# A decoder layer's down projection for two of three token groups, done as seven block products

## The chip, the cores and the metric

One core of one Trainium2 chip. The metric is the device time of one execution in microseconds (us), as the median of several runs. A profile of one execution stands beside it; its "span" runs from the first to the last instruction of the program.

## What is computed

One decoder layer over 1056 tokens (1024 of a prompt, 32 of eight decoded sequences), width 1024, in float32. In short, from the reference:

```python
h = _rms(x, n_mix_pre); z = h @ w_in                     # q, k, v, pooling input
mix = concat([attention(q, k, v), pooling(u)]) @ w_out
x = x + _rms(mix, n_mix_post)
f = _rms(x, n_ffn_pre)
f = (silu(f @ w_gate) * (f @ w_up)) @ w_down             # 1024 -> 2816 -> 1024
x = x + _rms(f, n_ffn_post)
x = x + sigmoid(x @ w_ple_gate) * (p @ w_ple)            # "PLE", p has 256 columns
```

The change concerns `@ w_down`: 2816 hidden columns, which are 22 chunks of 128, times a 2816 x 1024 matrix.

## The kernel before

**Layout.** Activations lie transposed: 128 partitions are 128 columns of the model, and the free dimension holds tokens. The tokens are three groups (0, 1, 2) of 352. A tile of half a group's state is 128 x 4 x 352 = 128 x 1408 elements. All such tiles come from one pool of 27 slots (`act_tile`, `half`, `A_SLOTS`).

**Precision.** Each operand X is split into hi (a rounded copy, made by ScalarE, line 171) and lo (X - hi, made by VectorE, line 172); a product takes three matmuls, hi·hi + hi·lo + lo·hi (`gemm`). One matmul is 128 x 128 weights against 128 x 352 tokens.

**Weights.** `w_load` brings raw weights (512 KB, 128 x 1024) on SP's DMA queue into one of three raw tiles (`wr`, `W_RAW`). Splits go into eight tiles (`wp`). The list ITEMS holds all weights of the feed-forward part in the order of use; `need(k)` makes item k and those up to four ahead (`LOOK`). An item is "direct" (split all of it: `wh`, `wl`), "half" (split its second half: `w`), "small" (for the PLE embedding) or "sums" (below).

**Groups 0 and 1 together ("the pair").** Their gate, up and PLE gate products are already done in a seven-product form of a 2 x 2 block matrix product (Winograd's variant of Strassen's). The weights are four blocks of 4 x 128 rows; the tokens four blocks (two halves of the rows by two groups). `w_sums` (line 1025) makes the weight blocks' four sums on POOL, in place in the raw tiles; then ScalarE and VectorE split them (`sh`, `sl`). `f7` holds seven token operands B11, B21, B22 and T1 to T4, each as hi and lo (14 tiles). `seven` runs the products one after another, 12 matmuls into one PSUM bank each, and VectorE adds the banks up into the four results C11, C12, C21, C22. With eight PSUM banks, TensorE stops when VectorE is too late. For a chunk, seven products make gate and up for both groups: 84 matmuls where the plain way takes 96.

**Group 2** goes the plain way (`direct`: 24 matmuls into one bank).

**Order.** TensorE's instructions stay in the order of the program from line 988 on; a scheduler orders the other engines' instructions when the program is built, and each engine then takes its own in that order. WALK is the list of (slab, groups), a slab being two chunks: six slabs of group 2, eleven slabs of the pair, the other five of group 2. For each slab gate and up of its chunks are made; the hidden values are split into `hid` (`hid_put`); and inside the next slab's first chunk `downs` runs the slab's down products: for each group and each of eight output blocks m, six matmuls (two chunks, three each) into a bank, which VectorE adds to the output tile `os_` (line 1130, the first time ScalarE copies). That is 22 x 8 x 3 = 528 matmuls for a group.

**Chains.** The work between the big products (norms, residual sums, the making of `f7`, of `fs[2]` for group 2, of `x27` and `x2s` for PLE) is written as generators (`ffn_steps`, `pair_steps`, `one_steps`), which `turn` advances between products by estimated costs, so that it lies beside the products. `t_sum` (line 984) makes T1 to T4 from the state on POOL, `sum_halves` (line 357 to 360) and `squares_into` (line 816) the sums of squares, for groups 0 and 1 on POOL. `finish` runs what is left of a chain.

**The PLE stage** has four steps of seven products for the pair (`ple_pair`), the last down products of group 2 after the first of them, and then eight plain steps for group 2 (`ple_one`).

Of the kernel before, what the change touches and what calls it, by code (L numbers as in the profile page):

```python
# [10 lines left out]
F32 = mybir.dt.float32  # L11
# [5 lines left out]
P = 128  # L17
# [19 lines left out]
SLAB = 2  # L37
NSLAB = FFC // SLAB

AHEAD = 6  # L40
# [17 lines left out]
A_SLOTS = 27  # L58
# [3 lines left out]
def trunk_kernel(  # L62
# [9 lines left out]
    w_dn,  # L72
    w_pg,
# [145 lines left out]

    WALK = [(s, (2,)) for s in range(AHEAD)]  # L220
    WALK += [(s, (0, 1)) for s in range(NSLAB)]
    WALK += [(s, (2,)) for s in range(AHEAD, NSLAB)]
    LAST = {g: max(n for n, (_, gs) in enumerate(WALK) if g in gs) for g in range(G)}
# [6 lines left out]
    def direct_item(src, shape):  # L230
        return item("direct", add_plan(src, shape))
# [4 lines left out]
    def half_item(src):  # L236
        return item("half", add_plan(src, [P, KC, P]))

    def dn_items(n):
        return [direct_item(w_dn[WALK[n][0], j], [P, SLAB, 512]) for j in range(2)]  # L240

    WGU, WD = [], []
    for s, gs in WALK:
        pairs_of = []
        for i in range(SLAB):
            c = SLAB * s + i
            jg = direct_item(w_gu[c, 0], [P, KC, P])
            if 0 not in gs:
                ju = direct_item(w_gu[c, 1], [P, KC, P])
            if i == 0 and WD:  # L250
                WD[-1] = dn_items(len(WD) - 1)
            if 0 in gs:
                ju = half_item(w_gu[c, 1])
            js = item("sums", jg, ju) if 0 in gs else None
            pairs_of.append((jg, ju, js))
        WGU.append(pairs_of)
        WD.append(None)


    WP2, WPE = [], [None] * KC  # L260
    for i in range(KC // 2):
        jg = direct_item(w_pg[2 * i], [P, KC, P])
        ju = half_item(w_pg[2 * i + 1])
        js = item("sums", jg, ju)
        WP2.append((small_item(w_ple[i]), jg, ju, js))
        if i == 0:
            WD[-1] = dn_items(len(WALK) - 1)
    wp = WP2[-1][0]
    LATE = (6, 7, *range(6))
    for m in LATE:  # L270
        if m < 6 and m % 2 == 0:
            wp = small_item(w_ple[m // 2])
        WPE[m] = wp, direct_item(w_pg[m], [P, KC, P])
# [47 lines left out]
    def rstd_steps(acc):  # L321

        n = acc.shape[1]
        sm = bank()
        for i in range(TB):
            at = min(i * P, n - P)
            mm(sm[:, i : i + 1], acc[:, at : at + P], ones[:, 0:1], start=True, stop=True)
        sd = spool.tile([P, TB], F32, tag="sd", name=nm("sd"))  # L330
        fix(se.activation(sd, sm[:, :TB], AF.Sqrt, bias=epst, scale=1.0 / D))
        fix(ve.reciprocal(sd, sd))
        hl = spool.tile([P, 2, TB], F32R, tag="hl", name=nm("hl"))
        fix(ve.tensor_copy(hl[:, 0], sd))
        fix(ve.tensor_tensor(hl[:, 1], sd, hl[:, 0].bitcast(F32), op=ALU.subtract))
        dgs = []
        for h in range(2):
            dg = spool.tile([P, TB, P], F32R, tag="dg", bufs=4, name=nm("dg"))
# [12 lines left out]
    def acc_tile(g):  # L351
        return spool.tile([P, NS[g]], F32, tag=f"acc{g}", bufs=1, name=nm("acc"))

    def sum_halves(sqs, g, eng=ve):

        a, b = sqs
        fix(eng.tensor_tensor(a, a, b, op=ALU.add))
        fix(eng.tensor_tensor(a[:, 0:2, :], a[:, 0:2, :], a[:, 2:4, :], op=ALU.add))
        acc = acc_tile(g)
        fix(eng.tensor_tensor(acc, a[:, 0, :], a[:, 1, :], op=ALU.add))  # L360
        return acc
# [23 lines left out]
    xs, acc1, r1 = [[None] * 2 for _ in range(G)], [None] * G, [None] * G  # L385
# [18 lines left out]
    def x_sums(g):  # L404
        acc1[g] = sum_halves([xr[g, h] for h in range(2)], g)
# [402 lines left out]
    acc = [acc_tile(g) for g in range(G)]  # L808
# [119 lines left out]
    def ffn_steps(g):  # L928
# [8 lines left out]
        acc2 = sum_halves(ys[g], g, ve if g == 2 else ge)  # L937
        yield (20, 6) if g == 2 else (0, 45)
        r = yield from rstd_steps(acc2)
        for h in range(2):  # L940
# [32 lines left out]
    f7 = {}  # L973

    def t_sum(name, b7, c0, c1, to):
# [8 lines left out]
        ge.tensor_tensor(out, a, b, op=ALU.subtract)  # L984
# [22 lines left out]

    hid = [None] * G

    new_hid = [None] * G  # L1010

    def hid_put(g, slot, ht):
        split(new_hid[g][:, slot, :], new_hid[g][:, SLAB + slot, :], ht)

# [41 lines left out]
    def seven(items, x7, done):  # L1056

        ig, iu, is_ = items
# [21 lines left out]
    def gate_up_pair(items, slot, pending):  # L1080
# [3 lines left out]
        def done(which, c):  # L1084
# [3 lines left out]
            if which == "C11":  # L1088
                if pending:
                    pending()  # L1090
                for g in (0, 1):
                    if slot == 0:
                        new_hid[g] = half(g, F32R, "hid")
            for g, a, b in ((0, "C21", "C11"), (1, "C22", "C12")):
                if which == ("C21", "C12")[g]:
                    ve.tensor_tensor(t[a], t[a], t[b], op=ALU.mult)
                    hid_put(g, slot, t[a])

        seven(items, f7, done)

    def gate_up_one(items, slot, pending):
        ig, iu, _ = items
        wg = need(ig)
        sl = tmp(N, "sl")
        se.activation(sl, direct(wg, fs[2]), AF.Silu)
        wu = need(iu)
        ve.tensor_tensor(sl, sl, direct(wu, fs[2]), op=ALU.mult)
        if slot == 0:
            new_hid[2] = half(2, F32R, "hid")
        hid_put(2, slot, sl)  # L1110
        if pending:
            pending()

    os_ = [None] * G

    def down(n, m, g):
        wh, wl = need(WD[n][m // 4], 0 if n == len(WALK) - 1 else LOOK)
        cols = slice((m % 4) * P, (m % 4 + 1) * P)
        ps = bank()
        v = ps[:, : NS[g]]  # L1120
        gemm(v, [(wh[:, k, cols], wl[:, k, cols], hid[g][:, k, :], hid[g][:, SLAB + k, :]) for k in range(SLAB)])
        turn(6)
# [3 lines left out]
        if (g, m) not in begun:  # L1126
            begun.add((g, m))
            se.copy(o, v)
        else:
            ve.tensor_tensor(o, o, v, op=ALU.add)  # L1130

    begun = set()
    x2 = [[None] * 2 for _ in range(G)]
# [3 lines left out]
    acc3 = [None] * G  # L1137
    x2d = [[dpool.tile([P, 4, NS[g]], F32, name=nm("x2d")) for _ in range(2)] for g in range(2)]

    def last_down(n, m, g):  # L1140
        down(n, m, g)
        if m == 0:
            acc3[g] = acc_tile(g)
        squares_into(acc3[g], os_[g][m // 4][:, m % 4, :], m == 0, ve if g == 2 else ge)
# [47 lines left out]
    def downs(n):  # L1192
        gs = WALK[n][1]
        hid[:] = old_hid
        for half_m in (range(4), range(4, KC)):
            for g in gs:
                for m in half_m:
                    (last_down if n == LAST[g] else down)(n, m, g)
        if n == LAST[0]:
            share[0] = 0.5  # L1200
            chain(pair_steps(), 19)
        if n == LAST[2]:
            chain(one_steps(), 40)

    for n, (s, gs) in enumerate(WALK):
        if n == AHEAD:
            finish(list(chains))
        old_hid = list(new_hid)
        for i in range(SLAB):
            pending = (lambda: downs(n - 1)) if i == 0 and n else None  # L1210
            (gate_up_pair if 0 in gs else gate_up_one)(WGU[n][i], i, pending)
    finish(list(chains))
    share[0] = 0.5


# [15 lines left out]
    def ple_pair(i):  # L1231

        wp, *items = WP2[i]
# [5 lines left out]
        def done(which, c):  # L1239
# [3 lines left out]
            embed(wp, xm[g][:, m % 4, :], m, g, c)  # L1243
# [3 lines left out]
    def ple_one(m):  # L1247
        wp, w = WPE[m]
# [4 lines left out]
    old_hid = list(new_hid)  # L1253
    for i in range(KC // 2):
        ple_pair(i)
        if i == 0:
            downs(len(WALK) - 1)
    finish(list(chains))
    for m in LATE:
        ple_one(m)  # L1260
# [14 lines left out]
def _layout(i):  # L1275
# [28 lines left out]
        "w_dn": wd.reshape(NSLAB, SLAB, P, 2, 512).transpose(0, 3, 2, 1, 4),  # L1304
# [43 lines left out]
```

## Time and profile before

| | |
|---|---|
| median of 3 runs | 1118.83 us (1117.93 to 1118.85) |
| the profiled execution | 1120.06 us |
| its span | 1117.9 us |
| TensorE's granted clock, mean | 0.997 |
| matmuls | 7099 |
| POOL's sums of weights (line 1025) | 104 of 1.30 to 1.36 us |
| loads of weights for w_gate, w_up, w_down | 132 of 512 KB, 3.3 us each |

How to read the profile: PE is TensorE's matmuls, PEld its weight loads, DVE is VectorE, ACT ScalarE, POOL GpSimd, SP the queue that issues most DMAs. A row of a group gives line, engine, operation, output tile <- input tiles, shapes, count, then busy us, mean ns of one, and the idle time just before them with what ended it. A row of a wait gives who waited for what: us in total, times, longest. A row of the timeline gives start, length, engine, line, operation and, in brackets, the idle time before it. Matmuls overlap in the profile, so that the time of one says less than their number in a stretch.

### The profile page before, as it was taken

The page shows a single profiled execution, that of the slowest core. Times are in us where ns is not written, and L with a number is a line of the kernel's source. Part 1 is how long each engine was busy: PE and PEld are TensorE (multiplying, and loading weights), DVE is VectorE, ACT ScalarE, POOL GpSimd, SP SyncE. Part 2 cuts the span into 40 slices and gives each one's busy share as a digit, 9 for nine tenths or more (in the row PEclk, how much of TensorE's full clock was granted, in tenths as well). Part 3 has the DMA queues.
Part 4 walks back from the last instruction along what each step waited for, and adds up shares of the span by engine and source line. Part 5 has one row for each costly group of instructions (what it writes and reads, how often), then busy time and mean ns, then how long its engine had stood idle before and what let it go on. Part 6 is the DMA issues. An engine that isn't in the chain of part 4 may idle for free.

```text
span 1117.9 us, 18031 instructions
## 1 busy us (share of the span) xinstructions
PE 1102.0 (99%) x7099; PEld 1084.3 (97%) x7099; DVE 818.8 (73%) x1298; ACT 476.6 (43%) x834; POOL 259.7 (23%) x200
## 2 busy tenths in 40 slices
PE   9999999999999999999999999999999999998998
PEld 8999988899999999999999999999999999998998
DVE  6766478877989957477677677677677788867973
ACT  7322377665555433533233233233233644443441
POOL 0054132100223212212212212212211503113200
PEclk9999999999999999999999999999999999999999
DMA  8121311542543333222122222122123555472261
GB/s 288 57 70 57 108 57 32 202 146 93 183 168 132 116 101 105 68 85 76 66 86 77 66 86 76 65 87 76 63 90 100 185 191 210 133 254 75 94 206 64
DMA packets 42421, 125.53 MB, mean 112 GB/s; under 512 B 4932, under 2 KB 15460, under 8 KB 42336
## 3 DMA queue, kind: packets, MB, share of 16 engines
q1 hardware_dynamic: 41008, 122.61, 32.4%
q10 hardware_dynamic: 1328, 1.77, 0.5%
q8 instruction: 56, 0.92, 0.3%
q14 instruction: 29, 0.24, 0.1%
HBM read 111.37 MB, written 12.99 MB: 111 GB/s over the span
## 4 chain that ended last, share of the span: by engine, by line
PE 93%; DVE 4%; DMA 2%; POOL 1%; issue 1%; ACT 0%; SPq 0%; DVEq 0%; POOLq 0%; ACTq 0%
PE b L126 92%; DVE wl L172 1%; PE b L120 1%; DMA a<-in_dmask_dram 1%; POOL wr L1025 0%; DVE fl L172 0%; DVE hid L172 0%; DMA xr<-in_x_dram 0%; DMA wr<-in_w_gu_dram 0%; DVE dg L340 0%; DVE acc L816 0%; DVE mx L659 0%; DVE a L767 0%; DVE o L1130 0%; DVE y L944 0%
## 5 line engine op out<-in xcount | busy, mean ns | idle before, releaser
L126 PE MATMUL b<-hid,wh 128*128 128x352 f32 x1056 | 252.6, 322 | 1.6 <-DVE hid L172 1.2
L172 DVE TENSOR_TENSOR wl<-wr,wh 128x1024 fp32r<-128x1024 f32 (+1 forms) x148 | 195.7, 1323 | 43.5 <-ACT wh L171 33.6
L171 ACT CAST wh<-wr 128x1024 fp32r<-128x1024 f32 (+1 forms) x148 | 152.4, 1031 | 159.0 <-PE b L126 108.7
L126 PE MATMUL b<-fh,wh 128*128 128x352 f32 x624 | 202.7, 325 | 2.5 <-DVE o L1130 2.5
L126 PE MATMUL b<-fh,wl 128*128 128x352 f32 x624 | 201.2, 322 | 0.0
L126 PE MATMUL b<-fl,wh 128*128 128x352 f32 x624 | 201.0, 322 | 0.0
L126 PEld LDWEIGHTS b<-hid,wh 128*128 128x128 f32 x1056 | 182.7, 188 | 2.3 <-DVE hid L172 1.5
L126 PE MATMUL b<-hid,wl 128*128 128x352 f32 x528 | 169.3, 321 | 0.0
L1025 POOL TENSOR_TENSOR wr<-wr 128x512 f32<-128x512 f32 x52 | 67.8, 1303 | 431.2 <-DVE w L172 373.7
L126 PE MATMUL b<-fh,sh 128*128 128x352 f32 x416 | 134.3, 323 | 0.0
L126 PE MATMUL b<-fl,sh 128*128 128x352 f32 x416 | 133.4, 321 | 0.0
L126 PE MATMUL b<-fh,sl 128*128 128x352 f32 x416 | 133.4, 321 | 0.0
L1130 DVE TENSOR_TENSOR o<-o,b 128x352 f32<-128x352 f32 x240 | 112.7, 517 | 14.6 <-PE b L126 14.4
L126 PEld LDWEIGHTS b<-fh,wh 128*128 128x128 f32 x624 | 117.7, 189 | 3.1 <-DVE o L1130 3.1
L126 PEld LDWEIGHTS b<-fl,wh 128*128 128x128 f32 x624 | 118.1, 189 | 0.0
L126 PEld LDWEIGHTS b<-fh,wl 128*128 128x128 f32 x624 | 117.8, 189 | 0.0
L171 ACT CAST sh<-wr 128x1024 fp32r<-128x1024 f32 x52 | 54.2, 1045 | 131.3 <-POOL wr L1025 129.9
L126 PE MATMUL b<-h,wh 128*128 128x352 f32 x480 | 104.9, 324 | 1.0 <-ACT h L392 0.8
L172 DVE TENSOR_TENSOR sl<-wr,sh 128x1024 fp32r<-128x1024 f32 x52 | 63.6, 1223 | 56.0 <-ACT sh L171 54.5
L126 PEld LDWEIGHTS b<-hid,wl 128*128 128x128 f32 x528 | 99.1, 188 | 0.0
L126 PEld LDWEIGHTS b<-h,wh 128*128 128x128 f32 x480 | 81.5, 188 | 2.2 <-ACT h L392 1.1
L126 PEld LDWEIGHTS b<-fl,sh 128*128 128x128 f32 x416 | 78.2, 188 | 0.0
(173 smaller groups left out, 1890.1 us busy)
## 6 DMA issues: line engine op xcount, KB each, us to landing
wr<-in_w_gu_dram SPq DMA_DIRECT2D x88, 512.0 KB, 3.3
wr<-in_w_dn_dram SPq DMA_DIRECT2D x44, 512.0 KB, 3.3
wr<-in_w_pg_dram SPq DMA_DIRECT2D x16, 512.0 KB, 3.6
x<-in_x_dram SPq DMA_DIRECT2D x6, 704.0 KB, 7.6
x1d<-x SPq DMA_DIRECT2D x6, 704.0 KB, 3.4
x<-x1d SPq DMA_DIRECT2D x6, 704.0 KB, 6.5
out_y_dram<-yo SPq DMA_DIRECT2D x24, 176.0 KB, 1.9
wr<-in_w_out_b_dram SPq DMA_DIRECT2D x8, 512.0 KB, 3.3
```

The lines of the kernel that those rows point to most:

```text
L120: ins = te.transpose(out, src, ident)
L126: ins = te.matmul(*args, **kw)
L171: fix(se.copy(hi, src))
L172: fix(ve.tensor_tensor(lo, src, hi.bitcast(F32), op=ALU.subtract))
L1025: ge.tensor_tensor(out, a, b, op=op)
L1130: ve.tensor_tensor(o, o, v, op=ALU.add)
```

## The change

A slab is now four chunks, five slabs and a rest of two chunks (`REST`). The order is written out as a list STEPS of small steps.

- **Pair's down products.** For the pair a slab's hidden values are kept in float32 (`hidf`); when the slab's four chunks are there, `h_operands` makes seven operands `h7` from them (128 x 2 x 352 each; four sums and seven splits). The slab's down weights are, for each half j of the outputs, two raw tiles of 512 KB in the block order that `seven_items` takes: one direct, one half, one sums. `do_dn_pair` runs seven products for each j, each as two groups of 6 matmuls, and adds each into one of seven accumulators of its own (`accp`), in which all five slabs are summed up; so the combination of the seven into the four results is made once, at the end, by seven additions of 128 x 1408 on VectorE (`do_combine`). `do_dn_pair` of a slab stands after the second and third chunk of the next slab. The rest of two chunks goes the plain way (`do_dn_rest`).
- **Group 2's down products** take four chunks into a bank (12 matmuls), so that there is one addition to `os_` where there were two.
- **Group 2's state away.** Its normed state is stored to DRAM (`fsd`) when it is made, its partial output (`osd`) after its third slab; both are loaded again behind the pair's chunks, and the state split anew (`do_reload`, `do_reload_sums`). The pool of tiles has 30 slots; the tiles for sums of squares (`acc_rows`) and for the norm's diagonal (`dg2`) come from it.
- **Sums on VectorE.** `t_sum`, `sum_halves` and `squares_into` of groups 0 and 1 run on VectorE in place of POOL.

Group 2 has twelve chunks before the pair and ten behind it, as it had.

```diff
-SLAB = 2
+SLAB = 4
 NSLAB = FFC // SLAB
-AHEAD = 6
+REST = FFC - SLAB * NSLAB
+AHEAD = 3
-A_SLOTS = 27
+A_SLOTS = 30
...
+    for s in range(AHEAD):
+        for i in range(SLAB):
+            s_one(s, i)
+            if s:
+                s_dn_one(s - 1, i)
+    step("spill")
+    for s in range(NSLAB):
+        for i in range(SLAB):
+            s_pair(s, i)
+            if s == 0 and i < 2:
+                s_dn_one(AHEAD - 1, 2 * i, 2 * i + 1)
+                if i == 1:
+                    step("spill_sums")
+            if s and i in (1, 2):
+                s_dn_pair(s - 1, i - 1)
+    s_pair(NSLAB, 0)
+    s_pair(NSLAB, 1)
+    step("reload")
+    for j in range(2):
+        s_dn_pair(NSLAB - 1, j)
+    step("combine")
+    for s in range(AHEAD, NSLAB):
+        for i in range(SLAB):
+            s_one(s, i)
+            if s > AHEAD:
+                s_dn_one(s - 1, i)
+            if (s, i) == (AHEAD, 1):
+                s_dn_rest(0, 1)
...
-        acc2 = sum_halves(ys[g], g, ve if g == 2 else ge)
+        sum_halves(ys[g], acc[g])
...
+                    nc.sync.dma_start(fsd[h], ys[g][h])
...
-        ge.tensor_tensor(out, a, b, op=ALU.subtract)
+        ve.tensor_tensor(out, a, b, op=ALU.subtract)
...
+    def h_operand(name, src):
+        t = act_tile([P, 2, 2, N], F32R, "hp")
+        split(t[:, 0], t[:, 1], src)
+        h7[name] = t[:, 0], t[:, 1]
+
+    def h_sum(name, out, a, b):
+        ve.tensor_tensor(out, a, b, op=ALU.subtract)
+        h_operand(name, out)
+
+    def h_operands():
+        b11, b21, b12, b22 = (hidf[g][:, 2 * k : 2 * k + 2, :] for g in (0, 1) for k in range(2))
+        h_operand("B11", b11)
+        h_operand("B21", b21)
+        h_operand("B22", b22)
+        h_sum("T1", b11, b12, b11)
...
+    def do_dn_pair(s, j, items):
+        ia, ib, is_ = items
+        for at, which, h, x in (
+            (1, ia, 0, "B11"),
+            (2, ia, 1, "B21"),
+            (4, ib, None, "T4"),
+            (6, is_, "S2", "T2"),
+            (7, is_, "S3", "T3"),
+            (5, is_, "S1", "T1"),
+            (3, is_, "S4", "B22"),
+        ):
...
+            for r in range(2):
+                ps = bank()
+                gemm(ps[:, :N], [(w[0][:, 2 * c + r, :], w[1][:, 2 * c + r, :], xh[:, c, :], xl[:, c, :]) for c in range(2)])
+                turn(6)
+                o = accp[at][:, 2 * j + r, :]
+                if s:
+                    ve.tensor_tensor(o, o, ps[:, :N], op=ALU.add)
+                else:
+                    se.copy(o, ps[:, :N])
+
+    def do_combine():
+        for a, b in ((2, 1), (1, 6), (7, 1), (1, 5), (1, 3), (4, 7), (7, 5)):
+            ve.tensor_tensor(accp[a], accp[a], accp[b], op=ALU.add)
+        os_[0] = [accp[2], accp[4]]
+        os_[1] = [accp[1], accp[7]]
...
+    def do_reload():
+        for h in range(2):
+            t = half(2, s="fr")
+            nc.sync.dma_start(t, fsd[h])
+            fs[2][h] = f_operand(t, 2)
```

More of the change, by code (lines that the diff above doesn't have):

```diff
@@ L260, in trunk_kernel, with seven_items, step, s_one @@
-    WP2, WPE = [], [None] * KC
+    def seven_items(a1, a2, small=None):
+        jg = direct_item(a1)
+        more = () if small is None else (small_item(small),)
+        ju = half_item(a2)
+        return (jg, ju, item("sums", jg, ju), *more)
+    STEPS = []
+    def step(kind, *args):
+        STEPS.append((kind, args))
+    def s_one(s, i):
+        c = SLAB * s + i
+        step("one", s, i, (direct_item(w_gu[c, 0]), direct_item(w_gu[c, 1])))
+    def s_pair(s, i):
+        c = SLAB * s + i
+        step("pair", s, i, seven_items(w_gu[c, 0], w_gu[c, 1]))
@@ L404, in x_sums @@
     def x_sums(g):
[L405 removed]
+        sum_halves([xr[g, h] for h in range(2)], acc1[g])
     def u_load(c, h):
@@ L806, in out_pool @@
         se.copy(ys[g][0][:, m, :], ps[:, : NS[g]])
-    acc = [acc_tile(g) for g in range(G)]
+    acc = acc_rows()
     def squares_into(acc_g, src, first, eng=ve):
@@ L973, in trunk_kernel @@
     f7 = {}
+    fsd = [dpool.tile([P, 4, N], F32, name=nm("fsd")) for _ in range(2)]
     def t_sum(name, b7, c0, c1, to):
@@ L1136, in trunk_kernel, with do_dn_rest @@
     pls = [None] * G
-    acc3 = [None] * G
     x2d = [[dpool.tile([P, 4, NS[g]], F32, name=nm("x2d")) for _ in range(2)] for g in range(2)]
[L1140 to L1144, printed above, removed]
+    acc3 = []
+    def do_dn_rest(gs, its):
+        if not acc3:
+            acc3.extend(acc_rows())
+        for g in gs:
+            hi, lo = hid[g, NSLAB]
+            for m in range(KC):
+                wh, wl = need(its[m // 4], 1)
+                cols = slice((m % 4) * P, (m % 4 + 1) * P)
+                ps = bank()
+                gemm(ps[:, :N], [(wh[:, c, cols], wl[:, c, cols], hi[:, c, :], lo[:, c, :]) for c in range(REST)])
+                turn(6)
+                squares_into(acc3[g], o_add(g, m, ps[:, :N]), m == 0)
+        if 2 in gs:
+            chain(one_steps(), 40)
+        else:
+            share[0] = 0.5
+            chain(pair_steps(), 19)
     def x2_steps(g, operand):
@@ L1190, in one_steps @@
         yield 6, 0
[L1192 to L1213, printed above, removed]
     def embed(wp, xm, m, g, sg):
@@ L1251, in ple_one @@
         embed(wp, x2[2][m // 4][:, m % 4, :], m, 2, sg)
[L1253 to L1260, printed above, removed]
+    do = {
+        "one": do_one,
+        "pair": do_pair,
+        "dn_one": do_dn_one,
+        "dn_pair": do_dn_pair,
+        "dn_rest": do_dn_rest,
+        "combine": do_combine,
+        "spill": do_spill,
+        "spill_sums": do_spill_sums,
+        "reload": do_reload,
+        "ple_pair": do_ple_pair,
+        "ple_one": do_ple_one,
+    }
+    for kind, args in STEPS:
+        if kind == "ple_pair" and args[0] == 0:
+            finish(list(chains))
+            share[0] = 0.5
+        do[kind](*args)
 _OUTS = [
```

179 lines of the change are left out of this document (98 added, 81 removed).

## The prediction, made before the run

> **What bounds the kernel now.** I read the page first (busy shares, the chain that ended last), then the whole list of what TensorE waited for, then the stretch in which groups 0 and 1 pass gate, up and down.
>
> ```profile
> span 1117.9 us, 18031 instructions
> PE 1102.0 (99%) x7099; PEld 1084.3 (97%) x7099; DVE 818.8 (73%) x1298; ACT 476.6 (43%) x834; POOL 259.7 (23%) x200
> PE 93%; DVE 4%; DMA 2%; POOL 1%; issue 1%; ACT 0%; SPq 0%; DVEq 0%; POOLq 0%; ACTq 0%
> PE b L126 <- DVE o L1130: 2.9, 3, 2.2
> PE b L126 <- ACT w L171: 2.2, 1, 2.2
> ```
>
> The kernel is TensorE: 93% of the chain, and the longest waits sum to a few us. What matters is what one matmul costs, and the matmul's own 322 ns does not tell it, because matmuls overlap. I take it from the pace of the pair stage (the columns are stretch, length, then busy time and count of PE, PEld, DVE, ACT, POOL, then granted clock and DMA):
>
> ```profile
> 460.00:920.00 460.00, 460.00 (x2898) 460.00 (x2897) 327.62 (x523) 163.84 (x241) 116.77 (x90) 1.00 0.27 90
> 527.70:569.66 41.96, 41.96 (x266) 41.96 (x265) 29.51 (x49) 13.67 (x20) 10.64 (x9) 1.00 0.23 76
> L126 PE MATMUL b<-hid,wh 128*128 128x352 f32 x1056 | 252.6, 322 | 1.6 <-DVE hid L172 1.2
> ```
>
> 460/2898 = **0.159 us per matmul**, without a gap and at clock 1.00. The second row is one period, a slab of two chunks for groups 0 and 1: 2×84 + 96 = 264 matmuls; VectorE is busy 29.5 of 42 us there (70%).
>
> **The change, part by part.** *Matmuls.* For four chunks and two groups the down projection takes 4×8×2×3 = 192 matmuls now and 7×2×2×2×3 = 168 afterwards. Five slabs: **120 fewer × 0.159 = −19.1 us**. Group 2 and the last two chunks keep their count. These are plain deletions from the list, so this term is the surest; all else decides whether TensorE can use it.
>
> *VectorE in a pair slab of four chunks* (TensorE: 504 × 0.159 = 80.1 us). Prices:
>
> ```profile
> L1130 DVE TENSOR_TENSOR o<-o,b 128x352 f32<-128x352 f32 x240 | 112.7, 517 | 14.6 <-PE b L126 14.4
> L172 DVE TENSOR_TENSOR sl<-wr,sh 128x1024 fp32r<-128x1024 f32 x52 | 63.6, 1223 | 56.0 <-ACT sh L171 54.5 <-PE b L126 1.4
> L172 DVE TENSOR_TENSOR w<-wr,w 128x512 fp32r<-128x512 f32 x33 | 22.7, 687 | 6.4 <-ACT w L171 6.4
> L172 DVE TENSOR_TENSOR hid<-c,hid 128x352 fp32r<-128x352 f32 x22 | 11.4, 519 | 0.1
> L358 DVE TENSOR_TENSOR xr<-xr 128x704 f32<-128x704 f32 x3 | 2.7, 892 | 0.1
> L1025 POOL TENSOR_TENSOR wr<-wr 128x512 f32<-128x512 f32 x52 | 67.8, 1303 | 431.2 <-DVE w L172 373.7 <-DMA wr<-in_w_gu_dram 36.1 <-DMA out_y_dram<-yo 19.4
> ```
>
> Back to back an addition of 352 costs 112.7/240 = 0.47. Start from 2×29.5 = 59.0. Gone: 32 additions (15.0), 8 splits of hid (4.2), 4 splits of down weights (4.9). New: 28 additions (13.2), 2×(1.22+0.69+2×1.22) = 8.7 for weights and their sums, and 11 operations of 704 in `h_operands` at 0.89 (9.8). Sum **66.6 of 80.1 us, 83%** against 70%. ScalarE (13.7 of 42) stays far from full. POOL goes from 16 to 24 sums per four chunks (21 to 32 us).
>
> *How the weights arrive* is the dearest unknown. After the change a step of seven products follows a step of seven products some 30 times (22 chunks and 10 halves of the output, less the first two, which still have group 2's products beside them); now 96 plain down matmuls (15.3 us) stand between pairs of them. A step takes 84×0.159 = 13.35 us and needs two raw tiles out of three. So the second raw tile of a step can be loaded only when the first one of the step before is split. That circle can be read off one slab:
>
> ```profile
> 568.14 0.62 ACT L171 CAST w<-wr 128x512 fp32r<-128x512 f32 x1 [0.48 <-PE b L126]
> 569.66 1.29 POOL L1025 TENSOR_TENSOR wr<-wr 128x512 f32<-128x512 f32 x1 [16.98 <-DVE w L172]
> 574.10 1.28 POOL L1025 TENSOR_TENSOR wr<-wr 128x512 f32<-128x512 f32 x1
> 575.41 1.05 ACT L171 CAST sh<-wr 128x1024 fp32r<-128x1024 f32 x1 [3.57 <-POOL wr L1025]
> 576.49 1.23 DVE L172 TENSOR_TENSOR sl<-wr,sh 128x1024 fp32r<-128x1024 f32 x1 [3.19 <-ACT sh L171]
> 534.54 1.22 DVE L172 TENSOR_TENSOR sl<-wr,sh 128x1024 fp32r<-128x1024 f32 x1 [3.19 <-ACT sh L171]
> 535.69 3.10 DVE L1130 TENSOR_TENSOR o<-o,b 128x352 f32<-128x352 f32 x7
> wr<-in_w_gu_dram SPq DMA_DIRECT2D x88, 512.0 KB, 3.3
> ```
>
> 568.14 to 577.72 is 9.6 us, and the load takes 3.3: **12.9 us per turn with no queue at VectorE, against 13.35 per step**; 0.45 us to spare. The rows of 534.54 and 535.69 also show how VectorE waits: it stood 3.19 us for a cast, and the seven additions behind it then ran in a burst; a slab later the same. Against this stands a reserve: the sums of a step are first used by its fourth product, 3×1.91 = 5.7 us after it begins, so weights may be about 5.7 us late before TensorE feels it. Bounds: with waits under 0.45 per turn nothing; at 1.5 us per turn 30×1.05 − 5.7 = 26 us. I take 0.55, nearer to the rows (splits of weights wait for their cast, not for VectorE): 30×0.1 = **+3 us**.
>
> *The slab's end.* `h_operands` puts 9.8 us on VectorE and seven casts on ScalarE (a cast of 704 next to nothing beside its half-empty list), ahead of the next step's half split and of its evictions. Eight PSUM banks at 1.91 us per product are 15 us of cover for the evictions; the weights' reserve is 5.7. What is late next is the half split, hence POOL's sums. Bounds: 0, if the reserve holds, to 9.8−5.7 = 4.1 per slab end; I take 1.5, five times: **+7.5 us**.
>
> *Sums from POOL to VectorE.* Rows, and what POOL does to VectorE meanwhile:
>
> ```profile
> L984 POOL TENSOR_TENSOR y<-y,y 128x1408 f32<-128x1408 f32 x4 | 17.2, 4289 | 39.1 <-DVE fl L172 26.5 <-DVE y L944 12.5
> L1154 DVE TENSOR_TENSOR o<-o,b 128x1408 f32<-128x1408 f32 x6 | 9.6, 1617 | 1.6 <-PE b L126 1.6
> L816 DVE TENSOR_TENSOR acc<-acc,sq 128x352 f32<-128x352 f32 x28 | 14.8, 534 | 8.8 <-ACT sq L815 8.8
> 365.82 7.53 POOL L984 TENSOR_TENSOR y<-y,y 128x1408 f32<-128x1408 f32 x2 [1.63 <-DVE fl L172]
> 366.74 3.54 DVE L172 TENSOR_TENSOR hid<-sl,hid 128x352 fp32r<-128x352 f32 x1
> 360.00:380.00 20.00, 18.83 (x118) 18.54 (x118) 20.00 (x14) 9.01 (x11) 11.64 (x3) 1.00 0.32 106
> 380.00:400.00 20.00, 20.00 (x127) 20.00 (x127) 17.36 (x25) 7.94 (x10) 0.00 (x0) 1.00 0.48 158
> 940.00:960.00 20.00, 17.84 (x108) 17.55 (x107) 18.56 (x15) 11.36 (x12) 11.99 (x3) 0.96 0.40 142
> ```
>
> A subtraction of 1408 takes 4.29 us on POOL, 1.62 on VectorE, and beside POOL a VectorE operation of 0.52 us took 3.54. So the four sums ahead of the pair stage cost VectorE about what they cost it now. TensorE lost 127−118 = 9 matmuls in 360 to 380; I take **−2 us** (0 to −3). Behind the pair stage VectorE gets four sums (6.5), 14 additions of squares (14×0.53 = 7.4) and the seven additions that combine the accumulators (7×1.62 = 11.3), and loses POOL's blocking, which cost 127−108 = 19 matmuls (3.0 us) at 940. Bounds −3 to +8; I take 0, since both sides are about equal. Cover for the combination: two chunks of group 2, 2×48×0.159 = 15.3 us; without it up to 11.
>
> By the Trainium skill (SBUF — State Buffer, Who interferes with whom) VectorE and GpSimd take a shared port pair in turn, for a whole instruction, when a VectorE addition has both inputs in SBUF. The trace agrees (the 3.54 us above). The rule speaks for this part and against the ten new sets of POOL sums; by it alone, 40 sums could block VectorE for up to 40×1.3 = 52 us, which is an estimate from that page's rule and a bound only.
>
> *Group 2's state in DRAM.* Eight more transfers of 704 KB on the one queue that brings the weights.
>
> ```profile
> x<-x1d SPq DMA_DIRECT2D x6, 704.0 KB, 6.5
> L172 DVE TENSOR_TENSOR fl<-x,fh 128x1408 fp32r<-128x1408 f32 x5 | 10.0, 2002 | 1.5 <-ACT fh L171 1.4
> L171 ACT CAST fh<-x 128x1408 fp32r<-128x1408 f32 x5 | 6.9, 1372 | 1.9 <-DVE x L1157 1.9
> ```
>
> Reload takes 6.5 + 1.4 + 2.0 = 9.9 us for a half and some 3.4 more for the second. The last two steps of seven (26.7 us) hide it: 0. If a load waits for a free slot, the weight loads behind it on the queue wait too; then up to 10 us, once. The stores are hidden likewise (DMA share 0.27).
>
> **The sum.** The profiled execution took 1120.06, 2.2 more than its span and 1.2 more than the median 1118.83. 1120.06 − 19.1 + 3 + 7.5 − 2 = 1109.5; less 1.2, about **1108**.
>
> **Rivals.** *1. The circle of three raw tiles sets the pace of the pair stage.* For: 12.9 of 13.35, two visits at an 83% busy VectorE in each turn. Against: now it never binds, since splits are let through first. At 1.5 us of waits +26, at the slab ends 5: 1120.06 − 19.1 − 2 + 31 − 1.2 = **1129**, slower. It decides from the wait w at which 30(w−0.45) − 5.7 + 7.5 = 21.1: w = 1.1 us, a step of 14.0 us. Stalls of several us also show a clock that falls:
>
> ```profile
> 1018.00:1022.00 4.00, 1.69 (x9) 1.10 (x8) 4.00 (x9) 2.90 (x7) 0.00 (x0) 1.00 0.32 116
> 1022.00:1026.00 4.00, 3.17 (x12) 3.17 (x13) 3.73 (x7) 1.00 (x2) 0.00 (x0) 0.64 0.60 197
> ```
>
> *2. VectorE itself becomes the bound,* by POOL's sums lying beside its operations of 704 and its products: 66.6 plus 10 us (a 0.52 us operation lasted 0.80 and 0.99 beside a sum) is 96% of 80. A loss of 5% of 400 us takes back the gain: **1118**, no change. Against:
>
> ```profile
> 1040.00:1060.00 20.00, 20.00 (x127) 20.00 (x126) 20.00 (x32) 9.56 (x13) 5.67 (x4) 1.00 0.31 103
> 570.52 0.80 DVE L1096 TENSOR_TENSOR u<-u,p 128x352 f32<-128x352 f32 x1 [0.56 <-ACT p L1087]
> 571.88 0.99 DVE L172 TENSOR_TENSOR hid<-u,hid 128x352 fp32r<-128x352 f32 x1 [0.55 <-ACT hid L171]
> ```
>
> There VectorE was busy without a gap, in steps of seven products, and TensorE lost nothing.
>
> *3. The pair's end comes too late:* combination, squares and sums push the pair's last operand past the first PLE product: +8 on the forecast, **1116**, still a small gain.
>
> **Chances.** Forecast 0.50 (its own range 1097 to 1115: no stall at all gives 1120.06 − 19.1 − 3 − 1.2 = 1097, the slab ends at 3 each give 1115); rival 1 0.26; rival 2 0.15; rival 3 0.09. Range 1097 to 1134, from no stall to rival 1 with w = 1.7; 1 in 10 is left out on each side. A measurement tells 0.2% (2.2 us) from no change: faster 0.56 (forecast 0.48, part of rivals 2 and 3), same 0.10, slower 0.34 (rival 1 and the worse part of 2).
>
> **What would show it.** Right: 6979 matmuls, VectorE about 83% in the pair stage, 127 matmuls per 20 us there but for dips behind each fourth chunk, and no POOL operation of 1408. Rival 1 shows as SP waiting for `sl` in front of every second weight load, TensorE waiting for `sl` or `sh`, and POOL's sums 14 us or more apart; rival 2 as VectorE over 95% with TensorE waiting for PSUM banks. I am wrong altogether if the reload holds the weight queue, or if TensorE idles where the pair stage begins or ends.

## The result, and the profile after

The changed kernel takes **1133.48 us** (median of 4 runs, 1132.01 to 1134.2) where the kernel before took 1118.84 beside it (4 runs, 1117.93 to 1120.15): ratio 1.0128 [1.0111, 1.0146], **slower by 14.6 us**. The forecast of 1108 us, faster, has the wrong sign; the time lies inside the range, near what rival 1 gave. The profiled execution took 1133.11 us, with a mean clock of 0.989 (0.997 before). Its page, and the waits of TensorE and of the SP queue (us in total, times, longest):

```profile
span 1131.3 us, 17864 instructions
PE 1097.9 (97%) x6979; PEld 1074.9 (95%) x6979; DVE 843.6 (75%) x1298; ACT 505.5 (45%) x863; POOL 262.4 (23%) x212
```

```profile
PE b L128 <- ACT sh L173: 12.2, 5, 3.3
PE b L128 <- DVE ap L1221: 4.5, 4, 3.4
PE b L128 <- DVE sl L174: 3.7, 6, 0.7
SPq L183 <- DVE sl L174: 467.7, 72, 16.9
```

The 120 matmuls are gone (7099 to 6979), yet the span grew by 13.4 us. TensorE now waits five times, up to 3.3 us, for `sh`: the cast of the weight sums that POOL makes. (Line 128 is the matmul, 173 the cast of a split and 174 its difference, 1054 POOL's sums, 1131 the sums of `h_operands`, 1158 the product that gives the hidden values, 1221 and 1223 the addition and the first copy into `accp`; in kernels of the experiments these numbers are up to a few lines higher.)

Where the time went shows in stretches, counted in matmuls. At the pace of before (126 per 20 us) 480 to 520 would hold 252, 520 to 820 would hold 1890, 820 to 880 would hold 378. Columns as in the prediction:

```profile
360.00:380.00 20.00, 20.00 (x128) 20.00 (x127) 18.87 (x20) 12.28 (x13) 0.00 (x0) 1.00 0.43 150
480.00:520.00 40.00, 35.66 (x218) 34.54 (x217) 22.05 (x30) 18.08 (x32) 15.84 (x12) 1.00 0.24 79
520.00:820.00 300.00, 288.59 (x1749) 284.53 (x1748) 214.35 (x325) 111.93 (x161) 118.03 (x84) 0.98 0.21 71
820.00:880.00 60.00, 51.30 (x295) 49.36 (x294) 50.95 (x77) 23.76 (x32) 19.11 (x12) 0.94 0.39 136
940.00:960.00 20.00, 20.00 (x130) 20.00 (x129) 14.11 (x20) 10.55 (x12) 0.00 (x0) 1.00 0.67 240
```

The first and the last row are the places where POOL's subtractions and squares had cost 9 and 19 matmuls: these losses are gone. Between them 34 matmuls are missing at the pair's **entry**, 141 in the **slabs** and 83 at the **exit** (last slab end, combination, reload): 258 × 0.159 = **41 us lost**, where before lost none.

One slab end, on ScalarE and VectorE, then POOL, then TensorE (start, length, and in brackets the idle time before):

```profile
647.97 2.15 ACT L173 CAST hp<-hf 128x704 fp32r<-128x704 f32 x3 [0.40 <-DVE hf L1158]
650.03 0.61 ACT L173 CAST w<-wr 128x512 fp32r<-128x512 f32 x1
...
661.23 1.99 ACT L173 CAST sh<-wr 128x1024 fp32r<-128x1024 f32 x2 [4.85 <-POOL wr L1054]
```

```profile
649.92 2.49 DVE L174 TENSOR_TENSOR hp<-hf,hp 128x704 fp32r<-128x704 f32 x3
652.32 0.89 DVE L1131 TENSOR_TENSOR hf<-hf,hf 128x704 f32<-128x704 f32 x1
653.13 0.69 DVE L174 TENSOR_TENSOR w<-wr,w 128x512 fp32r<-128x512 f32 x1
```

```profile
636.31 1.30 POOL L1054 TENSOR_TENSOR wr<-wr 128x512 f32<-128x512 f32 x1 [7.14 <-DVE w L174]
...
653.95 2.63 POOL L1054 TENSOR_TENSOR wr<-wr 128x512 f32<-128x512 f32 x1 [12.02 <-DVE w L174]
656.66 3.20 POOL L1054 TENSOR_TENSOR wr<-wr,wr 128x512 f32<-128x512 f32 x2
659.94 1.26 POOL L1054 TENSOR_TENSOR wr<-wr 128x512 f32<-128x512 f32 x1
```

```profile
662.33 0.66 PE L128 MATMUL b<-fh,sh 128*128 128x352 f32 x1 [2.72 <-ACT sh L173]
```

The half split `w` of the next step stands behind three casts of hidden operands (2.15 us) on ScalarE; its cast ends at 650.64, and its difference then stands until 653.13 behind VectorE's operations of 704. POOL cannot start its sums before that. The four sums then take 653.95 to 661.20, 7.25 us where those of the other steps between two slab ends take 5.4 to 5.9. Most of it is the first, which lies beside VectorE's operations: 2.63 us in place of 1.29 to 1.30. From start to start of POOL's sums a slab end has 17.6 us (636.31 to 653.95) where 13.35 are due: 4.3 more, and 1.6 for the longer sums (5.6 in the step before). So the sums come some 6 us late, and TensorE waits.

The wait is not the whole price. The same stretch by granted clock (the column before the last two):

```profile
660.00:680.00 20.00, 17.36 (x90) 16.91 (x91) 13.59 (x21) 7.84 (x11) 6.53 (x5) 0.83 0.24 76
662.00:664.00 2.00, 1.36 (x3) 0.91 (x4) 1.69 (x2) 2.00 (x3) 0.00 (x0) 0.50 0.00 0
664.00:666.00 2.00, 2.00 (x8) 2.00 (x8) 1.97 (x4) 0.52 (x2) 0.00 (x0) 0.50 0.75 236
666.00:668.00 2.00, 2.00 (x9) 2.00 (x8) 1.90 (x4) 0.97 (x2) 0.00 (x0) 0.50 0.84 260
```

From 662 to 668 the clock is at 0.50. The first row lacks 126 − 90 = 36 matmuls, 5.7 us, of which TensorE stood 2.6; the other 3 are the slow clock.

### The profile page after: what moved, and what is told of

Its sections match the earlier page's. It is cut to its first block, busy times and chain, and to the rows that moved or that the text cites. A ratio compares the mean times of both kernels' runs of the same rounds, so it can differ in the third digit from the quotient of the medians.

```text
span 1131.3 us, 17864 instructions
## 1 busy us (share of the span) xinstructions
PE 1097.9 (97%) x6979; PEld 1074.9 (95%) x6979; DVE 843.6 (75%) x1298; ACT 505.5 (45%) x863; POOL 262.4 (23%) x212
## 5 line engine op out<-in xcount | busy, mean ns | idle before, releaser
L1054 POOL TENSOR_TENSOR wr<-wr 128x512 f32<-128x512 f32 x72 | 101.9, 1415 | 650.3 <-DVE w L174 647.5
L173 ACT CAST wh<-wr 128x1024 fp32r<-128x1024 f32 (+1 forms) x138 | 142.0, 1030 | 153.7 <-PE b L128 75.1
L174 DVE TENSOR_TENSOR wl<-wr,wh 128x1024 fp32r<-128x1024 f32 (+1 forms) x138 | 168.0, 1218 | 33.7 <-ACT wh L173 32.6
L174 DVE TENSOR_TENSOR sl<-wr,sh 128x1024 fp32r<-128x1024 f32 x72 | 87.4, 1222 | 125.5 <-ACT sh L173 121.7
L173 ACT CAST sh<-wr 128x1024 fp32r<-128x1024 f32 x72 | 72.9, 1048 | 193.7 <-POOL wr L1054 193.7
L1054 POOL TENSOR_TENSOR wr<-wr,wr 128x512 f32<-128x512 f32 x72 | 102.2, 1420 | 5.6
L128 PE MATMUL b<-hid,wh 128*128 128x352 f32 x416 | 99.5, 322 | 0.0
L128 PEld LDWEIGHTS b<-fh,sh 128*128 128x128 f32 x416 | 81.1, 195 | 15.1 <-ACT sh L173 14.0
L128 PEld LDWEIGHTS b<-fh,sl 128*128 128x128 f32 x416 | 81.1, 195 | 5.6 <-DVE sl L174 5.6
L128 PE MATMUL b<-hp,sh 128*128 128x352 f32 x320 | 78.9, 329 | 7.5 <-DVE ap L1221 4.2
L128 PEld LDWEIGHTS b<-h,wh 128*128 128x128 f32 x480 | 82.7, 191 | 1.1 <-ACT h L426 0.6
```

What stands on the lines that cost most here:

```text
L128: ins = te.matmul(*args, **kw)
L173: fix(se.copy(hi, src))
L174: fix(ve.tensor_tensor(lo, src, hi.bitcast(F32), op=ALU.subtract))
L1054: ge.tensor_tensor(out, a, b, op=op)
```

## The experiments

**Theory A**: the burst of `h_operands` at each slab end. **Theory B** (rival 1): the ring of three raw tiles (the prediction's circle: load, half split, POOL's sums, split of the sums), in every step. A turn of the ring is the time from POOL's first sum of one step to its first sum of the next. They are told apart in the first four runs, whose expectations also name a **theory C**: VectorE is too busy in the pair stage as a whole. What these four left open gave theory D and rivals E and F; the expectations of the later runs name them. All ratios are against the kernel before, run on the same chip.

**1. no_operands.** Hidden operands are made for the first slab only; the later slabs use them again.

```diff
-        if s < NSLAB and i == SLAB - 1:
+        if s == 0 and i == SLAB - 1:
             h_operands()
```

> Left out: the making of the seven hidden operands for slabs 1 to 4 (11 VectorE operations of 704 and 7 casts each); their products use slab 0's operands, with as many matmuls. Theory A (the slab's end: these operations lie ahead of the next half split of weights on VectorE and ScalarE, and the weights' sums come too late once per slab): TensorE's waits of 2.7 to 3.3 us for the cast of the sums go, with the slow clock behind them, 6 to 8 us at each of four slab ends, so 1133.5 becomes 1102 to 1108. Theory B (the circle of three raw tiles is too slow in every step, 12.9 us plus waits against 13.35): the turns stay at 13.5 us or more and 1120 or more remains. Theory C (VectorE is the bound in the pair stage as a whole): 44 operations of 0.9 us go, 40 us of VectorE, and the time falls to about 1105 as well, but with VectorE's busy share in the pair stage having been near full before, which the profile shows as 72%.

Measured: 1105.63 us, 0.9867 [0.9852, 0.9882]. Its stretches, and the starts of POOL's sums, 16 turns apart:

```profile
480.00:520.00 40.00, 35.64 (x218) 34.52 (x217) 22.58 (x31) 18.11 (x32) 15.94 (x12) 1.00 0.24 79
520.00:820.00 300.00, 300.00 (x1890) 300.00 (x1889) 204.63 (x316) 106.07 (x151) 121.16 (x91) 1.00 0.25 83
820.00:880.00 60.00, 56.17 (x337) 55.36 (x336) 54.38 (x81) 24.39 (x35) 6.72 (x6) 0.97 0.49 166
```

```profile
573.20 1.29 POOL L1054 TENSOR_TENSOR wr<-wr 128x512 f32<-128x512 f32 x1 [7.73 <-DVE w L174]
...
787.07 1.30 POOL L1054 TENSOR_TENSOR wr<-wr 128x512 f32<-128x512 f32 x1 [7.36 <-DVE w L174]
```

The slabs lose nothing: 1890 of 1890 at clock 1.00. (787.07 − 573.20)/16 = 13.37 us per turn, just TensorE's 13.35. So B as worded, a ring too slow in every step, falls; A has its time. C forecast the same time, but with a VectorE near full, and it is busy 214.35 of 300 us in the changed kernel's slabs.

At the exit 41 matmuls stay lost, so these have another cause than these four bursts. The 34 of the entry stay too, but they say nothing against it: this run still makes the first slab's operands, and its burst lies just there.

```profile
478.39 2.63 POOL L1054 TENSOR_TENSOR wr<-wr 128x512 f32<-128x512 f32 x1 [12.01 <-DVE w L174]
486.79 0.43 PE L128 MATMUL b<-fh,sh 128*128 128x352 f32 x1 [0.79 <-ACT sh L173]
```

It is the same long turn as at the later slab ends (17.6 us from 460.83 to 478.39), and TensorE waits 0.79 and 0.68 us behind it. In the changed kernel this end cost 13 matmuls (90 from 480 to 496, 103 before), 2.1 us; the other 21 lie at two waits for ScalarE's first copies into `accp`.

**2. late_operands.** The same work one step later, behind the second product of the next slab's first chunk.

```diff
+            if which == "C11" and i == 0 and s:
+                h_operands()
...
-        if s < NSLAB and i == SLAB - 1:
-            h_operands()
```

> The same work as the changed kernel; the seven hidden operands of a slab are written into the program one step later, behind the call that asks for the next weights (in the first chunk of the next slab, after its second product), so that the next half split goes ahead of them. Theory A: the waits at the slab ends shrink from 3 us to under 1, 1105 to 1112. Theory B: no gain, 1130 to 1136. Theory C: no gain, 1130 to 1136.

Measured: 1134.0 us, 1.0124 [1.0109, 1.0139], no gain: A's forecast for this run, 1105 to 1112, failed, and those of B and C hold the time. TensorE's longest wait moved from `sh` to `sl`, and the long turn of POOL's sums moved by one: 670.23 − 651.64 = 18.6 us.

```profile
PE b L128 <- DVE sl L174: 16.3, 6, 3.4
```

```profile
651.64 1.81 POOL L1054 TENSOR_TENSOR wr<-wr 128x512 f32<-128x512 f32 x1 [9.23 <-DVE w L174]
...
670.23 1.30 POOL L1054 TENSOR_TENSOR wr<-wr 128x512 f32<-128x512 f32 x1 [11.07 <-DVE w L174]
```

The order of the burst and the half split alone does not decide: in both places tried some split of a turn stands behind the whole burst, here `sl`.

**3. four_raw.** A fourth raw tile; room for it comes from a sixth `tmp` tile and two constant tiles.

```diff
-W_RAW = 3
+W_RAW = 4
...
```

> Four raw tiles for weights in place of three, room for them from five temporaries in place of six and from constants that share a tile. A load then waits for the tile of a whole step before. Theory A: the half split still stands behind the operands' casts, so 1125 to 1132. Theory B: the circle is open, TensorE's waits for the sums go, 1100 to 1108. Theory C: 1130 to 1136.

Measured: 1125.14 us, 1.0051 [1.0034, 1.0067]; 8.3 us off, at the edge of the range that A gave (1125 to 1132) and outside those of B and C. A slab still takes 86 us (POOL's first sums after a slab end start at 562.25, 648.41, 734.58) where 80.1 would do; TensorE waits 9.0 us in all for `sh`. An earlier load alone does not make the splits earlier.

**4. sums_alone.** The kernel before, with only the sums of the state and the sums of squares put on VectorE.

```diff
-        acc2 = sum_halves(ys[g], g, ve if g == 2 else ge)
-        yield (20, 6) if g == 2 else (0, 45)
+        acc2 = sum_halves(ys[g], g)
+        yield 20, 6
...
-        ge.tensor_tensor(out, a, b, op=ALU.subtract)
+        ve.tensor_tensor(out, a, b, op=ALU.subtract)
...
```

> The kernel before with only the sums of groups 0 and 1 (the four differences twice, the sums of squares) on VectorE in place of POOL. The prediction's step: -2 us ahead of the pair stage and 0 behind it, 1117. By the changed kernel's trace, where 340 to 400 us and 900 to 1000 us show no matmul lost, -5 to -6: 1113. If POOL had hidden these sums for nothing, VectorE's extra 27 us would cost time: 1122 or more.

Measured: 1112.23 us, 0.9932 [0.9915, 0.9948]: **this part alone gives 8 us**, four times what the prediction took. In the two stretches that had held 118 and 108 matmuls:

```profile
360.00:380.00 20.00, 20.00 (x128) 20.00 (x127) 19.26 (x26) 9.47 (x12) 0.00 (x0) 1.00 0.46 148
940.00:960.00 20.00, 20.00 (x128) 20.00 (x127) 19.58 (x22) 10.32 (x12) 0.00 (x0) 1.00 0.52 171
```

VectorE does all of it and TensorE loses nothing there. The loss had run on beside these two rows: 340 to 400 holds 379 matmuls in place of 360, 940 to 980 holds 254 in place of 228, together 45 matmuls or 7.1 us of the 8.

**5 and 6. spread_operands, spread_four_raw.** The burst in four pieces, spread over the products of the slab's last chunk and the next slab's first; the second with four raw tiles as well. In these two kernels and in all_mended the first difference is written over b12 in place of b11, so that operands made after it have other values; the instructions are as large as meant.

```diff
...
+            if which == "C11" and i == 0 and s:
+                h_operands(3)
...
+            if s < NSLAB and i == SLAB - 1 and which in ("C11", "C22"):
+                h_operands(0 if which == "C11" else 1)
...
-            h_operands()
+            h_operands(2)
```

> All the work of the changed kernel; the making of a slab's hidden operands is cut into four pieces of 2 to 3.6 us of VectorE (one in the slab's last chunk, one in its half, one at its end, one in the next slab's first chunk) in place of one of 9.8. Theory D (three raw tiles leave the circle of weights no time to catch up, the run without operands turned once in 13.37 us without a stall; so a burst of VectorE work that delays one turn is lost, with the slow clock behind it): pieces fit beside POOL's sums, the slab takes 81 to 84 us in place of 87.6, 1105 to 1116. Rival E (the sum of VectorE's work per slab counts, wherever it lies): 1128 to 1135.

> The pieces of the run before and four raw tiles. Theory D: with a circle that can catch up (turns of 12.0 us were seen with four tiles) nearly no stall is left in the pair stage, 1100 to 1107. Rival E: like four tiles alone, 1122 to 1127.

Measured: 1139.1 us, 1.0145 [1.0104, 1.0186], and 1132.87, 1.0084 [1.0052, 1.0116]. The ranges of theory D and of rival E both failed; spreading is no better than the burst (1133.48, and 1125.14 with four raw tiles). In spread_operands VectorE has, beside POOL's sums:

```profile
656.08 3.73 DVE L1132 TENSOR_TENSOR hf<-hf,hf 128x704 f32<-128x704 f32 x2
```

```profile
655.86 1.29 POOL L1054 TENSOR_TENSOR wr<-wr 128x512 f32<-128x512 f32 x1 [9.24 <-DVE w L174]
657.23 3.73 POOL L1054 TENSOR_TENSOR wr<-wr,wr 128x512 f32<-128x512 f32 x2
661.04 1.83 POOL L1054 TENSOR_TENSOR wr<-wr 128x512 f32<-128x512 f32 x1
```

Two operations of 704 took 3.73 us in place of 2 × 0.89, and POOL's sums 7.0 in place of 5.4 to 5.9. The pieces had been moved out of the half split's way into the sums' way.

**7. plain_down_sums.** The burst whole, at its place; POOL's sums for the down weights left out (the raw weights are split as they are).

```diff
...
-            ge.tensor_tensor(out, a, b, op=op)
+            if not plain:
+                ge.tensor_tensor(out, a, b, op=op)
```

> Left out: POOL's four sums for each half of the down weights (40 operations); their splits and products run on the weights as they are. Two of six turns become 5.4 us shorter, the operands' burst stays as it is. Theory D: a turn that is late can catch up in these two, so the slab takes 80 to 84 us: 1100 to 1115. Rival E: VectorE's work is the same, 1128 to 1135.

Measured: 1104.38 us, 0.9835 [0.9795, 0.9876], as theory D said; rival E (1128 to 1135) failed. The first sum of a slab end still takes 2.62 to 2.64 us and its turn is still long; but the slabs hold 1874 of 1890 matmuls at clock 1.00:

```profile
520.00:820.00 300.00, 299.51 (x1874) 298.76 (x1873) 232.69 (x353) 125.48 (x178) 87.28 (x60) 1.00 0.25 80
```

How it is caught up can be read in the lead, from the start of the cast `sh` to the product that uses it first. In plain_down_sums, at a slab end and a turn later:

```profile
647.53 2.00 ACT L173 CAST sh<-wr 128x1024 fp32r<-128x1024 f32 x2 [4.92 <-POOL wr L1057]
654.21 1.03 ACT L173 CAST sh<-wr 128x1024 fp32r<-128x1024 f32 x1
```

```profile
649.69 0.32 PE L128 MATMUL b<-fh,sh 128*128 128x352 f32 x1
663.03 0.48 PE L128 MATMUL b<-hp,sh 128*128 128x352 f32 x2
```

The lead is 2.2 us at the slab end and 8.8 a turn later: a step without sums refills it. In the changed kernel it is 4.0 us ahead of the slab end (cast at 641.96, product at 645.92) and falls to 1.1 (661.23 and 662.33), with the wait; in no_operands it is still 6.3 at that slab end (645.31 and 651.60). The stall needs both: taking away **either** the burst or these sums takes it away.

**8. all_mended.** Spread pieces, four raw tiles, the first slab's copies into `accp` on VectorE, and the combination behind group 2's next chunk.

> Spread pieces and four raw tiles, and at the pair's two ends: the first slab's products are copied to the accumulators by VectorE in place of ScalarE (TensorE waited 2.9 us for those copies), and the seven additions that combine the accumulators are written behind group 2's next chunk. Theory D: 1097 to 1103. Rival E: 1120 or more.

Measured: 1133.13 us, 1.0086 [1.0052, 1.0121]. Theory D's range (1097 to 1103) failed, as in runs 5 and 6, with which it shares the spread pieces; the time lies in rival E's (1120 or more).

**9 and 10. down_sums_vector, down_sums_four_raw.** The complete computation: burst at its place, the four sums of the down weights on VectorE, the others on POOL; the second with four raw tiles.

```diff
...
-            ge.tensor_tensor(out, a, b, op=op)
+            (ve if plain else ge).tensor_tensor(out, a, b, op=op)
```

> All the work of the changed kernel; the four sums for each half of the down weights are made by VectorE in place of POOL (0.6 to 0.7 us each for 1.3). Two of six turns become 2.5 to 3 us shorter; VectorE gets 4.8 us per slab more, 89% of 80. Theory D (the circle of weights lacks time to catch up after the operands' burst; leaving these sums out gave 80.7 us per slab): the slab falls to 82 to 85 us, 1108 to 1122. Rival E (the sum of VectorE's work counts): slower, 1138 or more. Rival F (it was POOL slowing VectorE and the other way round that cost the time): the burst lies beside the sums of a gate step, which stay, so 1128 to 1134.

> The run before with four raw tiles. Theory D: 1102 to 1112. Rival E: 1128 or more. Rival F: 1120 to 1126, as with four raw tiles alone.

Measured: 1118.29 us, 0.9984 [0.9974, 0.9994], and **1110.89 us, 0.9916 [0.99, 0.9932]**. Between changed kernel and down_sums_vector lie some 15 us, though VectorE got more work: what costs is that POOL stands in the ring (its own latency and its lying beside VectorE are not separated). Theory D's forecasts held here, as in run 7, though not in runs 5, 6 and 8. E (1138 or more, then 1128 or more) and F (1128 to 1134, then 1120 to 1126) failed: it is neither the sum of VectorE's work nor the burst beside a gate step's sums alone. With the fourth tile a slab takes 82.7 us. Its stretch of slabs, and a slab end:

```profile
520.00:820.00 300.00, 295.58 (x1835) 292.45 (x1834) 241.07 (x370) 120.86 (x174) 88.06 (x60) 1.00 0.24 76
```

```profile
649.83 0.43 PE L128 MATMUL b<-fh,sh 128*128 128x352 f32 x1 [0.79 <-ACT sh L174]
651.09 0.43 PE L128 MATMUL b<-fh,sl 128*128 128x352 f32 x1 [0.67 <-DVE sl L175]
```

55 matmuls are missing in place of 141, and the mean clock is 1.00: the waits shown are under 1 us.

**11. late_four_raw.** The late burst with four raw tiles, to see whether the tile makes up for it.

> Operands written one step later, and four raw tiles. With three tiles the later place moved the long turn by one step and gained nothing, as the raw tile of the next half split was not there earlier. Theory D: with the fourth tile it is there, so the split goes ahead of the burst: 1105 to 1118. Rival E: 1122 to 1127, as four tiles alone.

Measured: 1126.33 us, 1.0054 [1.0039, 1.007]: not D's 1105 to 1118, but the range given for E, as four raw tiles alone. A slab takes 86 us, as with four_raw. In no experiment with all of POOL's sums and all operands did the slab come near 80.1.

**12. down_sums_ends.** down_sums_four_raw, with the copies into `accp` on VectorE and the combination behind group 2's next chunk.

```diff
-                    se.copy(o, ps[:, :N])
+                    ve.tensor_copy(o, ps[:, :N])
...
-    step("combine")
...
+            if (s, i) == (AHEAD, 0):
+                step("combine")
```

> Down sums on VectorE, four raw tiles, the first slab's products copied by VectorE, and the combining additions behind group 2's next chunk. The first slab's two waits for ScalarE's copies (2.9 us) go and the wait of 3.4 us at the pair's end shrinks: 4 to 8 us below the run with down sums and four raw tiles. If the waits at the two ends come from elsewhere (the reloaded state's splits, the slots), no change against that run.

Measured: 1111.97 us, 0.9929 [0.9909, 0.9949]: no gain. From 480 to 520 it holds 244 matmuls (238 without the edit), from 520 to 820 it holds 1826 (1835), from 820 to 880 it holds 327 (324). The waits for ScalarE's copies went; nearly as much came back elsewhere.

## Why the prediction was wrong, step by step

*Matmuls, −19.1: right.* The count is 6979, and no_operands and plain_down_sums run the slabs at 0.159 us each.

*VectorE in a pair slab, 66.6 of 80.1: right enough.* plain_down_sums, with all of VectorE's work and hardly a stall, has 232.69 of 300, that is 62 of 80.1 us. Rival 2 (VectorE full) is refuted: down_sums_four_raw has 241.07 of 300 and is faster.

*How the weights arrive, +3: the reading was right, the use of it wrong.* 12.9 us per turn and 13.35 per step were put down as a ring that mostly holds; it holds at 13.37 in no_operands. But the same 0.45 us is all by which a lost us can be won back: six turns of a slab regain under 3 us. In the changed kernel's trace the lead (described under run 7) stays between 3.2 and 4.1 us in the five turns from 590 to 646 us, between two slab ends.

***The slab's end*, +7.5: the step that failed.** It priced a burst at 1.5 us (0 to 4.1), as VectorE's 9.8 us less a reserve of 5.7. The runs give 27.9 us for the operands of four slabs, the second to the fifth (1133.48 to 1105.63): 141 matmuls in the slabs, three ends of 141/3 × 0.159 = 7.5 us each, and 83 − 41 = 42 at the exit, 6.7 for the fourth. Three things were missed. The reserve is there once: the first burst met a lead of 6.1 us (cast at 466.35, product at 472.44) and cost 2.1, near the 1.5 taken. At the later slab ends it is not there again: the lead ahead of them is 3.5 to 4.4 us, 6.3 without the bursts. The burst is longer for the ring than for VectorE's list: three casts on ScalarE ahead of the half split, and POOL's sums stretched from 5.6 to 7.25 us. And a wait of 2.7 us brings some 3 us at half clock; the prediction had shown a falling clock beside rival 1 and priced it nowhere.

*Rival 1* came near in time (1129) with half of the mechanism: the ring without slack is needed, as plain_down_sums shows, but it binds only behind the burst, not in every step. Its sign on record, SP waiting for `sl`, does not tell: it is there in the changed kernel (467.7 us, 72 times), but before too (341.5, 52 times) and in no_operands (437.9, 72 times), whose slabs lose nothing. *Rival 3* did not show: from 1000 to 1080, where the PLE stage begins, the changed kernel holds 473 matmuls, before 457.

*Sums from POOL to VectorE, −2: mis-sized.* Alone they give −8.0 (1120.26 to 1112.23). The prediction counted the 20 us with the deepest loss on each side (9 and 19 matmuls); with the stretches beside them it is 45 matmuls, 7.1 us. The other mistake was to set VectorE's new sums behind the pair stage (6.5 and 7.4 us) against the end of POOL's blocking as equals; VectorE had room for them.

*Reload, 0.* No wait that shows is for it: at the exit of no_operands TensorE's waits of 0.5 us or more are for VectorE's `p` and `ap`, up to 1.94 us. What the sum had at nothing are **entry and exit**, though idling at the pair's two ends stood among the signs of being wrong: 34 and 41 matmuls, 11.9 us, in no_operands too. At the entry TensorE waits there for `sh` and `sl` (0.79 and 0.68 us, behind the first burst) and twice for ScalarE's first copies into `accp` (1.41 and 1.49).

**The ledger.** −19.1 (matmuls) −8.0 (sums) +29.1 (183 matmuls, four bursts) +11.9 (entry with the first burst, and exit) = +13.9 us, against +14.6 measured. Without the four bursts it is −15.2, against −14.6 for no_operands. It closes less well than it looks: the 16 matmuls (2.5 us) that both kernels have more than before in 1000 to 1080 are not in it, so some 3 us are not located.

**What stays open.** Why a fourth raw tile alone recovers only 8 us: its splits stand on ScalarE and VectorE in program order among work that waits for a late TensorE, but no run separates that. Why down_sums_ends gains nothing at the exit, and what the exit's 41 matmuls are lost to in detail. That spreading fails through POOL beside VectorE was read in one place of the trace, not tested by itself. Among the kernels with the complete computation that beat the one before, sums_alone (0.9932), down_sums_four_raw (0.9916) and down_sums_ends (0.9929) have overlapping intervals, and down_sums_vector (0.9984) is behind them: the seven-product form of the down projection, mended, has not been shown to add to the sums' gain.

## What to carry to other kernels

A ring of buffers that turns in 12.9 us against a step of 13.35 is a chain that hardly refills its reserve. Here the lead softened the first burst only; price each later one, on any of the ring's engines, at its full delay, unless some step of the period is short enough to refill the lead. Read the lead itself (from the start of the last preparation to its first use) instead of working out a reserve from the order of the products. And where two steps of one change can be run apart, the one that looked small may carry the gain.

## What the runs showed of the hardware that was not expected

**The clock falls after short waits.** After a wait of 2.72 us it was 0.50 for 6 us. In four_raw shorter ones were enough:

```profile
656.88 0.43 PE L128 MATMUL b<-fh,sh 128*128 128x352 f32 x1 [1.66 <-ACT sh L174]
658.13 0.66 PE L128 MATMUL b<-fh,sl 128*128 128x352 f32 x1 [0.67 <-DVE sl L175]
```

```profile
656.00:658.00 2.00, 0.59 (x2) 0.30 (x2) 1.15 (x2) 2.00 (x3) 0.00 (x0) 0.98 0.00 0
658.00:660.00 2.00, 1.87 (x6) 1.87 (x7) 1.97 (x4) 1.58 (x3) 0.00 (x0) 0.50 0.41 121
```

Waits of 1.66 and 0.67 us stood close together here, and the clock is at 0.50; after 0.79 and 0.67, in down_sums_four_raw, it stayed at 1.00:

```profile
650.00:652.00 2.00, 1.33 (x8) 1.04 (x8) 2.00 (x2) 2.00 (x4) 0.00 (x0) 1.00 0.00 0
```

By the Trainium skill (TensorE: Matmul & The Clock Gate, HAM oscillation — how this bites in real kernels) the rule is to have no idle gap over some 3.4 us. The halving agrees; the length does not: here gaps of 2.7 and 1.7 us were followed by it, and the measurement decides.

**Both engines can be the slow one.** At the slab end of the changed kernel POOL's sum took 2.63 us for 1.3 beside VectorE, two of whose operations kept their 0.89 there (the one at 655.76 took 1.56); in spread_operands VectorE's pair took 3.73 for 1.78 and POOL's pair 3.73 for about 2.7. Both agree with the rule of the Trainium skill that the prediction cites (SBUF — State Buffer, Who interferes with whom), that the port pair is taken in turn. In these places the price was not in the blocked us alone: they fell into a ring without slack.
